# Nine more U tiles in the gate stage of a PEER layer, staged in memory, and a new pace for the gathered rows

## The chip, the cores and the metric

One core of one Trainium2 chip runs the whole program: TensorE (PE, with its weight loads shown apart as PEld), VectorE (DVE), ScalarE (ACT), GpSimd (POOL) and SyncE (SP, which here issues the plain DMAs), with 16 DMA engines shared by SP's queue and POOL's queue of gathered rows. The metric is device time in microseconds (us), median of several executions.

## The reference, cut to what matters

Two transformer blocks in a row; the change lies in the first block's PEER layer. Every token picks 16 of 16,384 experts in each of 8 heads, takes a gelu of its dot product with each expert's row of U, weights it by the gate, and sums the experts' rows of V:

```python
def peer(h, w_query, sub_keys, expert_u, expert_v):
    ...
    eidx = jnp.take_along_axis(cand_idx, pos, axis=-1)
    g = jax.nn.softmax(best, axis=-1)
    def one_block(args):
        xb, ib, gb = args
        u = expert_u[ib]
        a = jax.nn.gelu(jnp.einsum('thkd,td->thk', u, xb).astype(jnp.float32), approximate=False)
        w = (gb * a).astype(expert_v.dtype)
        return jnp.einsum('thk,thkd->td', w, expert_v[ib])
```

T is 512 tokens, D is 1024.

## The kernel before, in words

The program runs four phases: a (mixers of the first block), b (PEER), c and d (the second block). The diff touches phase b alone, `phase_b` (L887 on) with `peer_gates` (L1056 on).

For 384 of the 512 tokens (ND = 3 blocks of 128) the layer is computed densely. The 16,384 experts are cut into 128 tiles of 128. A **U tile** n is the gelu of U's tile times the tokens: the tile's weights are loaded (L227, `w_raw`, three buffers), split into two halves on ACT and DVE (L71 `w_hi`, L72 `w_lo`, two buffers each), and give 24 matmuls (8 chunks of D by three products of halves, L76 to L78, into `b_ups`, two PSUM buffers); ACT's gelu (L919) then writes the 128x384 activations. The first NX = 10 of them go into the room of x, the others into a pool of NAB = 36 buffers (`b_a`). A **V step** n (`weighted`, then `add_rows`) multiplies the activations by the gates (L973, `b_wfull`, which reads `b_g`, loaded for four n at once from the table `b_gd` in memory), splits the product (`b_wh`, `b_wl`, four buffers) and V's tile (`b_vraw`, three buffers, into `b_vh`, `b_vl`, two buffers), and adds 18 matmuls into six PSUM sums (`b_acc`).

The last 128 tokens go by **gathered rows**: POOL gathers, for expert k of every token, the rows of U by an indirect DMA into one of four 128x1024 buffers of x (L942), and DVE takes the dot products (L949), 128 times; then the same with V's rows, which DVE adds up in `b_accg` (L959), 128 times. These 256 steps are handed out beside the loop over n: by a table of paces, PACE a step of the loop.

```python
                due += 0 if n < NX else PACE if n < 128 - NAB else 1.2
                while done < min(int(due), 256):
                    next(gs)
```

Ahead of that loop stands the **gate stage** (`peer_gates`): it finds the experts and writes the dense gate table. Its last part is 12 chunks of 32 tokens: DVE makes one-hot matrices (L1225), PE multiplies them (L1234, L1235, `g_gp`, 64 matmuls of 128x128 a chunk), ACT copies the sums out (L1237, `g_sg`, two buffers), and SP writes 2 MB a chunk to `b_gd` (L1240). The stage calls `u_tile` 52 times on its way. After 46 tiles the buffers are all taken; tiles beyond that can be multiplied only as far as PSUM holds them until an old activation has been used.

Within each engine the build's scheduler sets the order of instructions from the program's order and its dependencies; gathered-row steps are kept in program order on DVE. The queues of SP, POOL, ACT and DVE run strictly in that order, so a waiting instruction holds those behind it.

Of the kernel before, what the change touches and what calls it, by code (L numbers as in the profile page):

```python
# [10 lines left out]
F32 = mybir.dt.float32  # L11
# [38 lines left out]
def bcast_rows(ap, n, parts=128):  # L50
    return bass.AP(tensor=ap.tensor, offset=ap.offset, ap=[[0, parts], [1, n]])
# [804 lines left out]
TD = ND * 128  # L856
# [3 lines left out]
NX = 10  # L860
NAB = 36
NLAST = 4
PACE = 2.72


def consts_b():
# [20 lines left out]
def phase_b(K):  # L887
    nc, tc, d = K.nc, K.tc, K.d
    V, S, PE = nc.vector, nc.scalar, nc.tensor
    with ExitStack() as st:  # L890
        pb = st.enter_context(tc.tile_pool(name="b_pb", bufs=1))
        hT = K.hT
        h2g = K.h2g
        eg = pb.tile([128, 128], I32, name="b_eg")
        gg3 = pb.tile([128, 128], F32, name="b_gg3")
        ag = pb.tile([128, 128], F32, name="b_ag")
        accg = pb.tile([128, 1024], F32, name="b_accg")
        ups = st.enter_context(tc.tile_pool(name="b_ups", bufs=2, space=PSUM))
        small = st.enter_context(tc.tile_pool(name="b_small", bufs=1))
        P = Proj(K, st, ups, pools=(K.ur, K.us))  # L900
        ab = st.enter_context(tc.tile_pool(name="b_ab", bufs=NAB))
        dram = st.enter_context(tc.tile_pool(name="b_dram", bufs=1, space=DRAM))
        gd = dram.tile([32, 128, TD // GT, 4 * GT], F32, name="b_gd")
        xd = K.xd
        room = K.x[:].rearrange("p b n -> p (b n)")

        acts = []

        def u_tile():
            n = len(acts)  # L910
            if n == 128:
                return
            hi, lo = P.weight(d["u"][n // 2, :, n % 2].rearrange("p k e -> p (k e)"))
            ps = ups.tile([128, NB, 128], F32, name="b_ups")[:, 0:ND].rearrange("p b n -> p (b n)")
            for k in range(8):
                ks = slice(k * 128, (k + 1) * 128)
                K.mm3(ps, (hi[:, ks], lo[:, ks]), (hT[0][:, k, :TD], hT[1][:, k, :TD]), k == 0, k == 7)
            a = room[:, n * TD:(n + 1) * TD] if n < NX else ab.tile([128, TD], F32, name="b_a")[:]
            S.activation(a, ps, AF.Gelu)  # L919
            acts.append(a)  # L920

        with ExitStack() as s1:
            peer_gates(K, s1, P, hT, small, gd, eg, gg3, u_tile)
        while len(acts) < NAB + NX:
            u_tile()

        with ExitStack() as s2:
            vps = s2.enter_context(tc.tile_pool(name="b_vps", bufs=1, space=PSUM))
# [36 lines left out]
            def weighted(n, halves):  # L965

                if n % 4 == 0:
                    g4s[n // 4] = gp.tile([128, TD // GT, 4, GT], F32, name="b_g")
                    nc.sync.dma_start(g4s[n // 4][:].rearrange("p c i t -> p c (i t)"), gd[n // 4])
                raw = vr.tile([128, 1024], F32, name="b_vraw")  # L970
                nc.sync.dma_start(raw[:], d["v"][n * 128:(n + 1) * 128, :])
                f = wf.tile([128, TD], F32, name="b_wfull")
                V.tensor_tensor(f[:].rearrange("p (c t) -> p c t", t=GT), acts[n].rearrange("p (c t) -> p c t", t=GT),  # L973
                                g4s[n // 4][:, :, n % 4], op=OP.mult)
                wh = wsp.tile([128, TD], F32R, name="b_wh")
                wl = wsp.tile([128, TD], F32R, name="b_wl")
                K.split(f[:], wh[:], wl[:])
                vh, vl = halves
                K.split(raw[:], vh[:], vl[:])
                return wh, wl, vh, vl  # L980

            def add_rows(n, t, b, hf):
                wh, wl, vh, vl = t
                bs, cs = slice(b * 128, (b + 1) * 128), slice(hf * 512, (hf + 1) * 512)
                K.mm3(acc[b][hf][:], (wh[:, bs], wl[:, bs]), (vh[:, cs], vl[:, cs]), n == 0, n == 127)

            def v_halves():
                return vs.tile([128, 1024], F32R, name="b_vh"), vs.tile([128, 1024], F32R, name="b_vl")

            def finish(b, xn, gf, gm, x):  # L990

                nc.sync.dma_start(x[:], xd[b])
                ss = small.tile([128, 2, 2], F32, name=f"b_fs{b}")
                y = K.x[:, b]
                for hf in range(2):
                    cs = slice(hf * 512, (hf + 1) * 512)
                    t = accg[:, cs] if b == ND else wf.tile([128, 512], F32, name="b_t")[:]
                    V.tensor_tensor(t, t if b == ND else acc[b][hf][:], K.gt2[:, cs], op=OP.mult)
                    V.tensor_tensor(x[:, cs], x[:, cs], t, op=OP.add)
                    S.activation(junk[:, cs], x[:, cs], AF.Square, scale=1 / 32, accum_out=ss[:, 0, hf:hf + 1])  # L1000
                    V.tensor_tensor(y[:, cs], x[:, cs], gf[:, cs], op=OP.mult)
                    S.activation(junk[:, cs], y[:, cs], AF.Square, scale=1 / 32, accum_out=ss[:, 1, hf:hf + 1])
                    yield
                v = small.tile([128, 2], F32, name=f"b_fv{b}")
                V.scalar_tensor_tensor(v[:, 0:1], ss[:, 0, 0:1], EPS, ss[:, 0, 1:2], op0=OP.add, op1=OP.add)
                V.scalar_tensor_tensor(v[:, 1:2], v[:, 0:1], EPS, ss[:, 1, 0:1], op0=OP.mult, op1=OP.add)
                V.tensor_tensor(v[:, 1:2], v[:, 1:2], ss[:, 1, 1:2], op=OP.add)
                V.tensor_scalar(v[:], v[:], 0.5, None, op0=OP.mult)
                r = K.rsqrt(small, v[:], 2, f"b_f{b}")
                yield  # L1010
                V.scalar_tensor_tensor(xn[:], y, r[:, 1:2], gm[:], op0=OP.mult, op1=OP.mult)
                yield
                K.turn(xn, b, hT, ups, "b_ups")
                S.activation(y, y, AF.Copy, scale=r[:, 0:1])
                yield

            gs = gather_steps()
            done, due = 0, 0.0
            last = []
            room = []  # L1020
            early = None
            for n in range(128):
                if n < 128 - NLAST:
                    t = weighted(n, v_halves())
                    for b in range(ND):
                        for hf in range(2):
                            add_rows(n, t, b, hf)
                else:
                    last.append((n, weighted(n, P.halves() if n < 130 - NLAST else v_halves())))
                if n >= NX:  # L1030
                    u_tile()
                due += 0 if n < NX else PACE if n < 128 - NAB else 1.2
                while done < min(int(due), 256):
                    next(gs)
                    done += 1
                if done == 256:
                    if early is None:
                        next(gs, None)
                        gf, gm, x = [P.raw() for _ in range(3)]
                        nc.sync.dma_start(gf[:], bcast_rows(d["g_final"], 1024))  # L1040
                        nc.sync.dma_start(gm[:], bcast_rows(d["g_mix"], 1024))
                        early = finish(ND, h2g, gf, gm, x)
                    next(early, None)
# [1270 lines left out]
def build(tc, d, out, phases="abcd"):  # L2314
# [3 lines left out]
    with ExitStack() as st:  # L2318
# [16 lines left out]
        with ExitStack() as s1:  # L2335
            if "a" in phases or "b" in phases:
                p2 = s1.enter_context(tc.tile_pool(name="p2", bufs=1))
                K.colsa = p2.tile([128, 27], F32, name="colsa")
                nc.sync.dma_start(K.colsa[:], d["colsa"])
                K.gt2 = p2.tile([128, 1024], F32, name="gt2")  # L2340
                K.A2 = p2.tile([128, 8], F32, name="A2")
                K.sh2 = p2.tile([128, 8], F32, name="sh2")
                K.h2g = p2.tile([128, 1024], F32, name="h2g")
                K.ur = s1.enter_context(tc.tile_pool(name="ur", bufs=3))
                K.us = s1.enter_context(tc.tile_pool(name="us", bufs=2))
                K.xd = s1.enter_context(tc.tile_pool(name="xd", bufs=1, space=DRAM)).tile([NB, 128, 1024], F32, name="xd")
            if "a" in phases:
                phase_a(K)
            elif "b" in phases:
                nc.sync.dma_start(K.gt2[:], bcast_rows(d["gt2_t"], 1024))  # L2350
                nc.sync.dma_start(K.A2[:], d["A2_t"])
                nc.sync.dma_start(K.sh2[:], d["sh2_t"])
            if "b" in phases:
                phase_b(K)
# [28 lines left out]
```

## Time and profile before

| | us |
|---|---|
| median of 3 runs | 2638.91 (2637.82 to 2639.2) |
| the profiled execution's own time | 2639.42 |
| its span in the trace | 2637.6 |
| gate stage, from the first key scores to the last g_gp matmul (PE) | 352 to 724 |
| from there to the first V matmul, PE idle | 724 to 740.6 |
| V loop with U tiles | 740.6 to 1430 |
| V loop without U tiles, to the last V matmul | 1430 to 1607 |

Times in the rows further below are us from the span's start. A matmul's shown length is longer than the spacing at which PE takes the next one, so the cost of a tile is read from start to start. "Idle <- X" names what ended an engine's idle time.

### The profile page before, as it was taken

To read this page: it belongs to the slowest core of one execution; us is meant where nothing else is said; L and a number is where in the kernel's file an instruction comes from. 1 tells how busy PE (TensorE), PEld (TensorE's weight loads), DVE (VectorE), ACT (ScalarE), POOL (GpSimd) and SP (SyncE) were. 2 spreads that over 40 slices of the span, in tenths; PEclk is the share of its full clock that TensorE was granted. 3 is DMA by queue.
4 is the path that set the end of the run, shared out by engine and by line. 5 is a ranking of instruction groups with operands and counts; after the bars stand their busy time and mean duration, and the time that the engine had idled before them with its cause. 6 is when DMAs were issued, how large, how long until landed. Compare 5 with 4: busy or idle time off the path is not lost. (4 is left out here: it accounts for less than half of the span.)

```text
span 2637.6 us, 43720 instructions
## 1 busy us (share of the span) xinstructions
PE 2491.0 (94%) x17112; PEld 2075.5 (79%) x17112; DVE 1784.1 (68%) x3778; ACT 919.6 (35%) x1607; POOL 379.6 (14%) x261
## 2 busy tenths in 40 slices
PE   6999999999879999999999998999999989989995
PEld 5887988998869999999998787888797856565554
DVE  6654789988847777878888997576753673333334
ACT  4532533455533333333333344343532412121112
POOL 0000000000004555545555420000000000000000
PEclk8999999999989999999999998898999999999998
DMA  6237122338868999998998973222133489999995
GB/s 244 73 115 241 57 92 81 112 118 253 244 237 300 328 323 322 330 325 314 328 327 322 353 269 117 80 81 72 62 115 116 179 328 401 409 404 386 400 390 213
DMA packets 183483, 623.92 MB, mean 237 GB/s; under 512 B 15846, under 2 KB 66406, under 8 KB 156650
## 3 DMA queue, kind: packets, MB, share of 16 engines
q1 hardware_dynamic: 146410, 486.87, 49.6%
q0 software_dynamic: 36864, 134.23, 14.6%
q8 instruction: 135, 2.21, 0.3%
q14 instruction: 74, 0.61, 0.1%
HBM read 591.55 MB, written 29.49 MB: 235 GB/s over the span
## 5 line engine op out<-in xcount | busy, mean ns | idle before, releaser
L72 DVE TENSOR_TENSOR w_lo<-w_raw,w_hi 128x1024 fp32r<-128x1024 f32 x228 | 278.2, 1220 | 250.1 <-ACT w_hi L71 247.0
L71 ACT CAST w_hi<-w_raw 128x1024 fp32r<-128x1024 f32 x228 | 238.5, 1046 | 579.5 <-issue 205.6
L78 PE MATMUL b_ups<-hT,w_lo 128*128 128x384 f32 x1024 | 347.3, 339 | 6.7 <-DVE w_lo L72 6.5
L76 PE MATMUL b_ups<-hT,w_hi 128*128 128x384 f32 x1024 | 349.6, 341 | 1.4 <-ACT x_sb L919 1.0
L77 PE MATMUL b_ups<-hT,w_hi 128*128 128x384 f32 x1024 | 346.2, 338 | 0.0
L942 POOL DMA_INDIRECT x_sb<-in_u_rows,b_eg x128 | 191.9, 1499 | 979.9 <-ACT b_wh L71 741.2
L76 PE MATMUL b_acc<-b_vh,b_wh 128*128 128x512 f32 x756 | 295.7, 392 | 17.7 <-ACT b_vh L71 17.7
L77 PE MATMUL b_acc<-b_vl,b_wh 128*128 128x512 f32 x756 | 296.7, 392 | 2.9 <-DVE b_vl L72 2.7
L78 PE MATMUL b_acc<-b_vh,b_wl 128*128 128x512 f32 x756 | 295.9, 391 | 0.0
L76 PE MATMUL p_acc<-w_hi,hT 128*128 128x256 f32 x896 | 256.4, 286 | 3.0 <-ACT hT L71 2.8
L77 PE MATMUL p_acc<-w_lo,hT 128*128 128x256 f32 x896 | 253.5, 283 | 1.4 <-DVE w_lo L72 1.3
L78 PE MATMUL p_acc<-w_hi,hT 128*128 128x256 f32 x896 | 253.1, 283 | 0.3 <-DVE hT L72 0.3
L942 POOL DMA_INDIRECT x_sb<-in_v,b_eg x128 | 187.4, 1464 | 199.6 <-DVE b_accg L959 167.0
L78 PEld LDWEIGHTS b_ups<-hT,w_lo 128*128 128x128 f32 x1024 | 194.2, 190 | 9.0 <-DVE w_lo L72 8.9
L76 PEld LDWEIGHTS b_ups<-hT,w_hi 128*128 128x128 f32 x1024 | 194.6, 190 | 6.6 <-ACT b_a L919 1.7
L77 PEld LDWEIGHTS b_ups<-hT,w_hi 128*128 128x128 f32 x1024 | 194.3, 190 | 3.0
L76 PEld LDWEIGHTS p_acc<-w_hi,hT 128*128 128x128 f32 x896 | 171.3, 191 | 18.8 <-issue 13.2
L76 PEld LDWEIGHTS b_acc<-b_vh,b_wh 128*128 128x128 f32 x756 | 142.8, 189 | 44.9 <-ACT b_vh L71 17.9
L77 PEld LDWEIGHTS p_acc<-w_lo,hT 128*128 128x128 f32 x896 | 172.0, 192 | 2.2 <-DVE w_lo L72 1.8
L1894 PE MATMUL f_hp<-f_w,f_X 128*64 128x512 f32 (+1 forms) x640 | 171.4, 594 | 0.7 <-DVE f_X L1847 0.6
L78 PEld LDWEIGHTS p_acc<-w_hi,hT 128*128 128x128 f32 x896 | 170.7, 191 | 1.4 <-DVE hT L72 0.8
L71 ACT CAST b_wh<-b_wfull 128x384 fp32r<-128x384 f32 x128 | 65.4, 514 | 298.8 <-PE b_acc L77 276.4
(660 smaller groups left out, 4916.2 us busy)
## 6 DMA issues: line engine op xcount, KB each, us to landing
f_w<-in_w SPq DMA_DIRECT2D x192, 1024.0 KB
w_raw<-in_u SPq DMA_DIRECT2D x128, 512.0 KB
b_vraw<-in_v SPq DMA_DIRECT2D x128, 512.0 KB
b_gd<-g_sg SPq DMA_DIRECT2D x12, 2048.0 KB
b_g<-b_gd SPq DMA_DIRECT2D x32, 768.0 KB
a_ar_t<-in_w_ada SPq DMA_DIRECT2D x32, 512.0 KB
w_raw<-in_w_tok SPq DMA_DIRECT2D x20, 512.0 KB
a_ar_t<-in_w_ada SPq DMA_DIRECT2D x8, 1024.0 KB
```

Of the source, the lines that this page charges most:

```text
L71: self.nc.scalar.copy(hi, src)
L72: self.nc.vector.tensor_tensor(lo, src, hi, op=OP.subtract)
L76: first = mm(ps, a[0], b[0], start=start, stop=False)
L77: mm(ps, a[0], b[1], start=False, stop=False)
L78: mm(ps, a[1], b[0], start=False, stop=stop)
L942: nc.gpsimd.indirect_dma_start(out=r, out_offset=None, in_=d[src], in_offset=bass.IndirectOffsetOnAxis(ap=eg[:, k:k + 1], axis=0))
L1894: last = PE.matmul(p, X[:, k], ts["w31", k // 2][:, c0:c0 + 512], start=k == 0, stop=k == 7, skip_group_check=True)
```

## The change

The nine tiles 46 to 54 are made by `ahead()` in the gate stage, and by a loop right behind it for those that are left: their gelu goes into one of two 128x384 pieces of `b_accg` (which the gathered rows need only much later), and SP writes each to a table `b_ud` in memory (192 KB a tile). In the V loop the steps n = 10 to 18, which used to make these tiles, read them back into a `b_a` buffer instead. The pace of the gathered rows is 1.435 a step for n = 10 to 18 and 2.87 up to n = 91, where it was 2.72 throughout: at n = 92 the count due is 9 x 1.435 + 73 x 2.87 = 222.4, before 82 x 2.72 = 223.0; from there both take 1.2 a step.

```diff
@@ -860,7 +860,8 @@
 NX = 10
 NAB = 36
 NLAST = 4
-PACE = 2.72
+NS = 9
+PACE = 2.87
@@ -905,24 +906,49 @@
         acts = []
+        first = NAB + NX
+        ud = dram.tile([NS, 128, TD], F32, name="b_ud")
+        ready = iter(range(NS))
+
+        def ahead():
+
+            i = next(ready, None)
+            if i is not None:
+                a = accg[:, i % 2 * TD:(i % 2 + 1) * TD]
+                product(first + i, a)
+                nc.sync.dma_start(ud[i], a)
 
         def u_tile():
             n = len(acts)
             if n == 128:
                 return
+            a = room[:, n * TD:(n + 1) * TD] if n < NX else ab.tile([128, TD], F32, name="b_a")[:]
+            if first <= n < first + NS:
+                nc.sync.dma_start(a, ud[n - first])
+            else:
+                product(n, a)
+            acts.append(a)
+
+        def product(n, a):
             hi, lo = P.weight(d["u"][n // 2, :, n % 2].rearrange("p k e -> p (k e)"))
...
-            a = room[:, n * TD:(n + 1) * TD] if n < NX else ab.tile([128, TD], F32, name="b_a")[:]
             S.activation(a, ps, AF.Gelu)
-            acts.append(a)
+
+        def filler():
+            if len(acts) < first:
+                u_tile()
+            else:
+                ahead()
 
         with ExitStack() as s1:
-            peer_gates(K, s1, P, hT, small, gd, eg, gg3, u_tile)
-        while len(acts) < NAB + NX:
+            peer_gates(K, s1, P, hT, small, gd, eg, gg3, filler)
+        while len(acts) < first:
             u_tile()
+        for _ in range(NS):
+            ahead()
@@ -1029,7 +1055,7 @@
                 if n >= NX:
                     u_tile()
-                due += 0 if n < NX else PACE if n < 128 - NAB else 1.2
+                due += 0 if n < NX else PACE / 2 if n < NX + NS else PACE if n < 128 - NAB else 1.2
```

The scheduler moves more than these lines say. **ACT at the end of the gate stage** (`g_sg` is the copy of gate sums, `w_hi` the split of a U weight, `b_accg` as a target is a gelu of `ahead`). Before:

```order
L1237 ACTIVATE g_sg<-g_gp 128x128x4 x4
L71 CAST w_hi<-w_raw 128x1024
L1237 ACTIVATE g_sg<-g_gp 128x128x4 x18
L71 CAST b_wh<-b_wfull 128x384 x2
L71 CAST b_vh<-b_vraw 128x1024
```

With the change:

```order
L1263 ACTIVATE g_sg<-g_gp 128x128x4 x4
L71 CAST w_hi<-w_raw 128x1024
L938 ACTIVATE b_accg<-b_ups 128x384
L1263 ACTIVATE g_sg<-g_gp 128x128x4 x2
L71 CAST w_hi<-w_raw 128x1024
L938 ACTIVATE b_accg<-b_ups 128x384
L71 CAST w_hi<-w_raw 128x1024
L938 ACTIVATE b_accg<-b_ups 128x384
L71 CAST w_hi<-w_raw 128x1024
L938 ACTIVATE b_accg<-b_ups 128x384
L71 CAST w_hi<-w_raw 128x1024
L71 CAST b_wh<-b_wfull 128x384 x2
```

The 18 copies stood in one run; now a tile's split and gelu lie between each four of them, and three more tiles behind the last. On PE the last 144 gate matmuls stood in one run, with the V matmuls right behind; now they stand as four times 32, each with a U tile of 24 matmuls behind it, then 16, then four U tiles and 16 matmuls of a fifth, and only then the first V matmul. So 8 and two thirds U tiles more stand ahead of the V loop (before, 48 stood there, two of them past the 46 buffers). Behind it come 21 V steps without a U tile, then one U tile a step up to n = 92; before, U tiles began after 5 and a half V steps and ended at n = 86.

**SP at the hand-over to the V loop** (`b_gd` the writes of the gate table, `b_ud` the writes of the nine tiles, `b_g` the first read of the gate table). Before:

```order
L227 DMA w_raw<-in_u 128x1024
L1240 DMA b_gd<-g_sg 128x32x128 x2
L969 DMA b_g<-b_gd 128x1536
L971 DMA b_vraw<-in_v 128x1024 x3
L969 DMA b_g<-b_gd 128x1536
```

With the change:

```order
L919 DMA b_ud<-b_accg 128x384
L227 DMA w_raw<-in_u 128x1024
L1266 DMA b_gd<-g_sg 128x32x128
L919 DMA b_ud<-b_accg 128x384 x2
L227 DMA w_raw<-in_u 128x1024
L995 DMA b_g<-b_gd 128x1536
L919 DMA b_ud<-b_accg 128x384
L997 DMA b_vraw<-in_v 128x1024 x3
L995 DMA b_g<-b_gd 128x1536
```

The first loads of V stand behind the ninth write of `b_ud` as well.

**DVE where the U tiles end** (`w_lo` is a U weight's split, `b_accg<-x_sb` a gathered-row step, `b_vl` the split of V, one a V step). Before:

```order
L72 TENSOR_TENSOR w_lo<-w_raw,w_hi 128x1024
L959 SCALAR_TENSOR_TENSOR b_accg<-x_sb,b_ag,b_accg 128x1024 x2
L72 TENSOR_TENSOR b_wl<-b_wfull,b_wh 128x384
L959 SCALAR_TENSOR_TENSOR b_accg<-x_sb,b_ag,b_accg 128x1024
L72 TENSOR_TENSOR b_vl<-b_vraw,b_vh 128x1024
L959 SCALAR_TENSOR_TENSOR b_accg<-x_sb,b_ag,b_accg 128x1024
L973 TENSOR_TENSOR b_wfull<-b_a,b_g 128x384
L959 SCALAR_TENSOR_TENSOR b_accg<-x_sb,b_ag,b_accg 128x1024 x2
L72 TENSOR_TENSOR b_wl<-b_wfull,b_wh 128x384
L973 TENSOR_TENSOR b_wfull<-b_a,b_g 128x384
L72 TENSOR_TENSOR b_vl<-b_vraw,b_vh 128x1024
L959 SCALAR_TENSOR_TENSOR b_accg<-x_sb,b_ag,b_accg 128x1024 x3
```

With the change:

```order
L72 TENSOR_TENSOR w_lo<-w_raw,w_hi 128x1024
L985 SCALAR_TENSOR_TENSOR b_accg<-x_sb,b_ag,b_accg 128x1024 x2
L72 TENSOR_TENSOR b_wl<-b_wfull,b_wh 128x384
L985 SCALAR_TENSOR_TENSOR b_accg<-x_sb,b_ag,b_accg 128x1024
L72 TENSOR_TENSOR b_vl<-b_vraw,b_vh 128x1024
L985 SCALAR_TENSOR_TENSOR b_accg<-x_sb,b_ag,b_accg 128x1024
L999 TENSOR_TENSOR b_wfull<-b_a,b_g 128x384
L72 TENSOR_TENSOR b_wl<-b_wfull,b_wh 128x384
L999 TENSOR_TENSOR b_wfull<-b_a,b_g 128x384
L72 TENSOR_TENSOR b_vl<-b_vraw,b_vh 128x1024
L985 SCALAR_TENSOR_TENSOR b_accg<-x_sb,b_ag,b_accg 128x1024
```

Before, up to three row steps a V step went on for some V steps after the last `w_lo`; now they drop to one in the step after it. At the other end, the ten V steps n = 11 to 20 of the change hold 16 row steps and no `w_lo` on DVE, and n = 21 to 24 hold 2, 2, 3 and 4 row steps, with a `w_lo` from n = 23 on.

## Rows read from the trace of the kernel before

**Rows 1.** Windows by stretch: length; busy PE, PEld, DVE, ACT, POOL; clock, DMA share, GB/s

```profile
707.00:724.00 17.00, 11.77 (x145) 9.63 (x143) 13.89 (x22) 10.44 (x19) 0.00 (x0) 0.90 0.86 254
724.00:740.60 16.60, 0.00 (x0) 0.00 (x0) 2.39 (x5) 1.88 (x3) 0.00 (x0) 0.55 0.87 285
740.60:747.00 6.40, 6.26 (x15) 4.51 (x16) 4.76 (x8) 1.93 (x3) 2.52 (x2) 0.56 0.93 339
...
765.00:1430.00 665.00, 664.85 (x3378) 605.81 (x3377) 519.46 (x663) 234.23 (x324) 319.09 (x209) 1.00 0.88 315
1430.00:1480.00 50.00, 47.25 (x199) 37.95 (x198) 44.12 (x46) 14.22 (x20) 25.38 (x21) 0.97 0.93 345
```

**Rows 2.** Windows of the tile b_ups alone, up to the first V matmul

```profile
440.00:740.60 300.60, 215.71 (x1152) 203.76 (x1152) 0.00 (x0) 22.33 (x46) 0.95 0.57 180
```

**Rows 3.** Timeline of PE in the V loop: start, length, engine, line

```profile
1202.48 0.34 PE L76 MATMUL b_ups<-hT,w_hi 128*128 128x384 f32 x1
...
1206.64 0.39 PE L76 MATMUL b_acc<-b_vh,b_wh 128*128 128x512 f32 x1
...
1210.73 0.34 PE L76 MATMUL b_ups<-hT,w_hi 128*128 128x384 f32 x1
```

**Rows 4.** Timeline of ACT in the gate stage's chunks with U tiles

```profile
674.03 1.05 ACT L71 CAST w_hi<-w_raw 128x1024 fp32r<-128x1024 f32 x1 [2.69 <-PE b_ups L77]
...
680.10 1.05 ACT L71 CAST w_hi<-w_raw 128x1024 fp32r<-128x1024 f32 x1 [2.69 <-PE b_ups L77]
```

**Rows 5.** Timeline of PE: the first gate matmul behind the last U tile

```profile
706.90 0.23 PE L1234 MATMUL g_gp<-g_o,g_oj 128*128 128x128 f16 x1
```

**Rows 6.** Timeline of SP's issues at the hand-over

```profile
716.75 7.29 SPq L1240 DMA_DIRECT2D b_gd<-g_sg  x2
733.64 0.33 SPq L969 DMA_DIRECT2D b_g<-b_gd  x1
734.02 1.77 SPq L971 DMA_DIRECT2D b_vraw<-in_v  x3
```

**Rows 7.** Timelines of DVE and of PE at the hand-over

```profile
738.05 1.03 DVE L973 TENSOR_TENSOR b_wfull<-x_sb,b_g 128x384 f32<-128x384 f32 x2 [16.16 <-DMA b_g<-b_gd]
...
740.62 1.65 PE L76 MATMUL b_acc<-b_vh,b_wh 128*128 128x512 f32 x3 [17.71 <-ACT b_vh L71]
```

**Rows 8.** Timeline of DVE in one step of the V loop

```profile
1207.79 1.23 DVE L72 TENSOR_TENSOR w_lo<-w_raw,w_hi 128x1024 fp32r<-128x1024 f32 x1 [2.32 <-ACT w_hi L71]
1208.94 2.60 DVE L959 SCALAR_TENSOR_TENSOR b_accg<-x_sb,b_ag,b_accg 128x1024 f32<-128x1024 f32 x2
1211.45 0.56 DVE L72 TENSOR_TENSOR b_wl<-b_wfull,b_wh 128x384 fp32r<-128x384 f32 x1
...
1213.12 1.22 DVE L72 TENSOR_TENSOR b_vl<-b_vraw,b_vh 128x1024 fp32r<-128x1024 f32 x1
1214.25 0.56 DVE L973 TENSOR_TENSOR b_wfull<-b_a,b_g 128x384 f32<-128x384 f32 x1
```

**Rows 9.** Windows of 10 us, columns as in rows 1

```profile
1470.00:1480.00 10.00, 10.00 (x46) 8.29 (x45) 9.30 (x11) 3.06 (x5) 3.74 (x4) 1.00 1.00 399
1480.00:1490.00 10.00, 10.00 (x46) 8.29 (x45) 9.66 (x15) 5.16 (x8) 4.59 (x3) 1.00 0.99 374
```

**Rows 10.** Waits, 760 to 1430, then 1430 to 1610: us, times, longest

```profile
DVE b_junkg L949 <- DMA x_sb<-in_u_rows,b_eg: 10.2, 10, 2.3
DVE b_accg L959 <- DMA x_sb<-in_v,b_eg: 5.1, 7, 2.1
...
PE b_acc L77 <- DVE b_vl L72: 2.7, 2, 1.9
```

**Rows 11.** DMA: queue of gathered rows (packets, MB, share); issues with their sizes

```profile
q0 software_dynamic: 36864, 134.23, 14.6%
...
b_vraw<-in_v SPq DMA_DIRECT2D x128, 512.0 KB
...
b_g<-b_gd SPq DMA_DIRECT2D x32, 768.0 KB
```

## The prediction

> **What bounds the kernel now.** I read the windows by stretch first. From 765 to 1430 PE is busy for 664.85 of 665 us at a granted clock of 1.00, while DVE works 519 us and the DMA engines are at 0.88 [rows 1]: in the V loop PE sets the pace. The hand-over into that loop is different. From 724 to 740.6 PE does nothing, and from 740.6 to 747 the clock is at 0.56, near the lower of its two levels (1.2 instead of 2.4 GHz), after that idle stretch [rows 1]. Before that, from 707 to 724, PE is busy for 11.8 of 17 us: the U tiles have run out (their buffers are full; 46 gelus, 1152 matmuls = 48 tiles [rows 2]), and DVE, at 13.9 us, makes the gates alone. So the time to be had lies between 707 and 747, in a core that has 80 U tiles still to make.
>
> The timelines say why PE is idle there. SP ends the issue of the last two gate writes at 724.0, can issue the first read of the table only at 733.6, and then the first loads of V at 734.0 [rows 6]; DVE gets its gates at 738.05 after 16.2 us of waiting, and PE starts at 740.62 [rows 7]. The wait is one of writing the table and reading it back, which PE could fill with anything that needs neither gates nor a free activation buffer. Nine activations put into memory are such work.
>
> **The unit prices.** A U tile costs PE 1206.64 - 1202.48 = 4.16 us, a V step 1210.73 - 1206.64 = 4.09 us [rows 3]. In the gate stage a U tile with 32 gate matmuls takes 680.10 - 674.03 = 6.07 us, and ACT waits there for PE [rows 4], so PE is the bound and 32 gate matmuls cost 1.91. On DVE, from start to start: `w_lo` 1.15, a row step 2.51 / 2 = 1.255, `b_wl` with one more row step 1.67, so `b_wl` 0.42; `b_vl` 1.13; `b_wfull` at most 0.56 [rows 8]. A V step without U and rows is 2.1 us of DVE.
>
> **The sum, against the profiled execution's 2639.4 us** (the median shown, 2638.9, is 0.5 lower).
>
> 1. *Work taken out of the loop.* By the order, 8.67 more U tiles stand ahead of the first V matmul. They cost the loop 8.67 x 4.16 = 36.1 us, all on PE's path there: **-36.1**. (Not nine: two of the tiles beyond 46 were already multiplied early, and the change also draws two thirds of a tile and one more from behind the nine.)
>
> 2. *The loop starts later.* From the end of the last U tile at 706.90 [rows 5] PE now has four times 6.07, half a gate block (0.95) and 4.67 x 4.16: it would end at 751.6. The gates are late too: the last gate matmul comes at 706.9 + 24.3 + 0.95 = 732.1 and the last write about 1 us later. With the 9.6 us from the end of issue to the table's read and the 7.0 from there to PE's start [rows 6, 7] that gives 749.7. The third path is SP's: the loads of V stand behind the ninth write, whose gelu comes with the end of the third tile after the gates, 732.1 + 12.5 + 0.5 = 745.1; V took 6.6 us from issue to PE's start [rows 6, 7], which makes 751.7. ACT splits one more U weight ahead of the first gates, which I allow 0.6 for. I take a start at 752.3, against 740.6: **+11.7** (9 to 14). The three paths meet within 2 us, so none leaves a large gap.
>
> 3. *The clock.* With PE at work until 752 there is no idle stretch ahead of the V loop. From 740.6 to 747 PE started 15 matmuls [rows 1] where at 4.09 / 18 = 0.227 us it starts 28 at full clock: **-2.9**.
>
> 4. *The end of the U tiles.* From 1430 to 1480 PE started 199 matmuls [rows 1] instead of 50 / 0.227 = 220: 4.8 us lost, with PE waiting for `b_vl` [rows 10]. It is the place where V steps had lost their U tile but still carried up to three row steps: DVE 2.1 + 3 x 1.255 = 5.9 us against PE's 4.09. In the new order the U tiles last until the pace drops. **-4.8** (0 to -4.8).
>
> 5. *The new stretch without U tiles.* The 21 V steps from 752 to about 838 give PE 4.09 us a step. Steps 11 to 20 carry 16 row steps: DVE 10 x 2.1 + 16 x 1.255 = 41.1 us against PE's 40.9, even; steps 21 and 22 with two each are 0.5 us too long apiece, then U tiles are back. DVE has two V buffers of lead, which may cover all; without it the single late steps add up. **+2** (0 to 6).
>
> 6. *DMA in that stretch.* Steps 8 to 20 (53.2 us) need 13 V tiles of 0.524 MB, 13 / 4 gate reads of 0.786, eight of the nine reads of 0.197 MB, 16 gathered steps of 134.23 / 256 = 0.524 MB [rows 11] and about one U tile: 19.8 MB, or 372 GB/s. The loop's average is 315 at a share of 0.88, but 399 and 374 were reached at shares of 1.00 and 0.99 with PE busy throughout [rows 1, 9]. At 399 it costs nothing, at 315 the stretch takes 62.9 us, 9.7 more. I take **+3**, nearer to the rows at full share.
>
> The Trainium skill, in "DMA: Bandwidth & Descriptors", Specifications, gives about 358 GB/s as the limit of memory for one core. The windows of 10 us at 399 and 374 [rows 9] do not agree with it as a ceiling. By the page the stretch would take 19.8 / 0.358 = 55.3 us and term 6 would be 2.1; by the first of those rows it would be 0.
>
> Steady steps afterwards (n = 23 to 91) cost nothing: DVE 2.1 + 1.15 + 2.87 x 1.255 = 6.9 us under PE's 8.25. Their cover is 1.4 us a step; rows made DVE wait only 15.3 us in 665 [rows 10]. The writes of `b_ud` (0.197 MB each) are hidden if they land within the two U tiles between uses of the same half of `b_accg`, 12.1 us; the last gate write, ten times as large, took 9.6. The nine extra gelus and nine DMA reads replace nine gelus and nine 512 KB loads in the loop; rows on ACT show no bound there.
>
> -36.1 + 11.7 - 2.9 - 4.8 + 2 + 3 = -27.1, so 2639.4 - 27.1 = 2612.3; less the 0.5 of the median, **2612 us**. With all costs at their good ends, -36.1 + 9 - 2.9 - 4.8 = -34.8 (2604); at their bad ends, -36.1 + 14 - 2.9 + 0 + 6 + 9.7 = -9.3 (2630).
>
> **The rivals.**
>
> *A. The DMA engines hold the stretch without U tiles.* At the loop's usual 315 GB/s term 6 is 9.7, and late rows on DVE's strict queue bring term 5 to 6: 2612 + 6.7 + 4 = 2623. For it: share 0.88 as an average leaves little. Against: rows 9.
>
> *B. The staging holds ACT.* A gelu waits for the write from the same half two tiles earlier; behind it on ACT stand the gate copies. Should each write take 15 us, as it may behind 2 MB gate writes at a DMA share of 0.86 [rows 1], seven waits of 15 - 12.1 = 2.9 us could add up to 20 us ahead of the loop, some of it hidden in term 2: 2612 + 12 = 2624.
>
> *C. Slower: gathered rows become the bound of the whole loop.* A steady step now moves 0.524 + 0.524 + 0.197 + 2.87 x 0.524 = 2.75 MB in 8.25 us, 333 GB/s, where 2.72 asked for 324. If the engines cannot go beyond the 315 of rows 1, a step takes 8.73 us, and 70 steps lose 34: 2612 + 34 = 2646. The point at which the gain is eaten is 27.1 / 70 = 0.39 us a step, or 2.75 / 8.64 = 318 GB/s. Against it: the 345 of 1430 to 1480 and the rows 9, and that waits for rows are short [rows 10].
>
> *D. The change does not fill the gap:* PE starts at 752 but U tiles wait there for weights, so the gain is only what ran beside the gates. A load of U then comes later than its tile, which SP's strict order allows, as each of those loads stands behind a write that waits for a gelu. Four tiles of 4.16 lost: 2612 + 17 = 2629.
>
> **How the numbers follow.** What can be told from no change here is 0.2%, 5.3 us. The forecast has 0.76, A 0.10, B 0.05, C 0.05, D 0.04. All of the forecast, and most of A, B and D, are faster by more than 2633.6 asks for: 0.89. A, B or D with another mishap end within 0.2%: 0.06. C is slower: 0.05. The range runs from the good ends, 2604, to 2628, which takes in A and B and most of the bad ends.
>
> **What would show it.** Right: 24-matmul U tiles among the gate matmuls from 707 to 732 and behind them to 751, no PE idle of more than 2 us there and the clock at full level; the first V matmul at 751 to 753; 56.67 tiles' U matmuls before it; about 86 us to the next U tile; no hole in PE's row where the U tiles end. Wrong: ACT's gelus waiting for DMAs from `b_accg`; fewer than 18 V matmuls in 4.3 us between 790 and 840 with the DMA share at 1; or more than 8.3 us for a steady step.

## The result and the profile after

The change takes 2604.8 us (median of 4 runs, 2601.3 to 2611.0) against 2639.05 before: ratio 0.988, 95% interval 0.9859 to 0.9901. The forecast was 2612 with a range of 2604 to 2628, so sign and time came out, the time near the good end. The profiled execution took 2603.84 us, its span 2602.0 (before 2637.6).

The windows by stretch of the change come first (length; busy PE, PEld, DVE, ACT, POOL; clock, DMA share, GB/s); they answer to [rows 1].

```profile
707.00:724.00 17.00, 17.00 (x163) 16.52 (x162) 13.32 (x20) 10.16 (x18) 0.00 (x0) 1.00 0.84 260
724.00:740.60 16.60, 16.60 (x129) 16.28 (x128) 7.23 (x9) 7.23 (x12) 0.00 (x0) 1.00 0.96 287
740.60:752.00 11.40, 11.40 (x68) 11.40 (x67) 2.77 (x3) 3.92 (x5) 0.00 (x0) 1.00 1.01 318
752.00:765.00 13.00, 10.87 (x49) 8.77 (x49) 11.59 (x19) 7.04 (x10) 4.06 (x2) 1.00 0.92 355
765.00:845.00 80.00, 79.94 (x355) 66.09 (x354) 62.01 (x91) 29.34 (x40) 27.77 (x21) 1.00 0.92 337
845.00:1395.00 550.00, 550.00 (x2802) 502.79 (x2801) 458.69 (x577) 193.90 (x268) 288.30 (x195) 1.00 0.93 340
1395.00:1445.00 50.00, 50.00 (x245) 44.29 (x244) 37.33 (x40) 16.03 (x24) 19.71 (x16) 1.00 0.80 284
```

The idle stretch of [rows 1] is full of work, the clock stays at its upper level (2.4 GHz) through the hand-over, the U-free steps (765 to 845) run without a hole, and so does the place where the U tiles end (1395 to 1445, where [rows 1] had 47.25 of 50 in 1430 to 1480). The window of the U tiles' PSUM tile alone answers to [rows 2]: 1360 matmuls, or 56.67 tiles, stand ahead of the first V matmul, as forecast from the order.

```profile
440.00:754.50 314.50, 252.69 (x1360) 239.32 (x1360) 0.00 (x0) 26.65 (x55) 0.98 0.60 186
```

The first 6.4 us of the V loop, against the 15 matmuls at a clock of 0.56 that [rows 1] has for the same length from 740.6:

```profile
754.60:761.00 6.40, 6.37 (x28) 5.28 (x29) 6.04 (x10) 3.55 (x5) 2.62 (x2) 1.00 0.83 316
```

The timelines of SP, DVE and PE at the hand-over answer to [rows 6, 7].

```profile
735.40 0.43 SPq L1266 DMA_DIRECT2D b_gd<-g_sg  x1
...
745.48 0.32 SPq L995 DMA_DIRECT2D b_g<-b_gd  x1
746.90 0.32 SPq L919 DMA_DIRECT2D b_ud<-b_accg  x1
747.27 1.94 SPq L997 DMA_DIRECT2D b_vraw<-in_v  x3
...
751.68 1.03 DVE L999 TENSOR_TENSOR b_wfull<-x_sb,b_g 128x384 f32<-128x384 f32 x2 [3.94 <-DMA b_g<-b_gd]
...
754.63 1.66 PE L76 MATMUL b_acc<-b_vh,b_wh 128*128 128x512 f32 x6 [2.13 <-ACT b_vh L71]
```

SP has issued the last gate write at 735.8; it can issue the read only at 745.5, and the table is there at 751.7. PE has stood still for 2.1 us when it starts at 754.6. The next lines are the waits from 755 to 1560 (us in total, times, longest), to be read beside [rows 10]. Rows make DVE wait longer than before (32.6 us in all, where [rows 10] has 15.3 up to 1430), but nothing of it reaches PE, whose only wait there is the start itself.

```profile
DVE b_junkg L975 <- DMA x_sb<-in_u_rows,b_eg: 22.6, 31, 2.5
DVE b_accg L985 <- DMA x_sb<-in_v,b_eg: 10.0, 14, 1.6
PE b_acc L76 <- ACT b_vh L71: 2.1, 1, 2.1
```

**One table for all kernels.** A whole run scatters by 10 us and more, so the traces are compared by marks that PE sets, read from the first and last starts of its tiles. Start: first `b_ups` matmul to first `b_acc`. Loop: first to last `b_acc`. Own work: what the loop's matmuls take by [rows 3], 2304 x 4.09 / 18 = 523.5 us for V and 4.16 / 24 for each U matmul left in the loop; lost is loop less own work. Tail: last `b_acc` to the first `f_tp`, none of which the change touches. The U matmuls ahead of the loop were counted for each kernel by the window shown above. The marks of a row come from one trace; two traces of the change differ by 0.7 us in start + loop.

| kernel | median us | start | loop | own work | lost | start + loop | tail |
|---|---|---|---|---|---|---|---|
| before | 2639.05 | 297.0 | 866.2 | 856.3 | 9.9 | 1163.2 | 465.4 |
| change | 2604.8 | 310.3 | 821.2 | 820.2 | 1.0 | 1131.5 | 460.1 |
| change again (e8) | 2609.6 | 310.9 | 821.3 | 820.2 | 1.1 | 1132.2 | 464.8 |
| e1 old pace | 2623.0 | 310.9 | 839.1 | 820.2 | 18.9 | 1150.0 | 460.6 |
| e2 six tiles | 2625.4 | 310.1 | 839.8 | 831.3 | 8.5 | 1149.9 | 463.8 |
| e3 twelve tiles | 2610.1 | 313.9 | 819.9 | 814.7 | 5.2 | 1133.8 | 476.7 |
| e4 writes on ACT | 2610.4 | 312.1 | 823.8 | 820.2 | 3.6 | 1135.9 | 465.5 |
| e5 DVE load | 2610.7 | 311.0 | 823.6 | 820.2 | 3.4 | 1134.6 | 463.4 |
| e6 DMA load | 2619.4 | 309.6 | 832.4 | 820.2 | 12.2 | 1142.0 | 464.9 |
| e7 clock fill | 2640.6 | 297.0 | 865.4 | 856.3 | 9.1 | 1162.4 | 465.5 |
| e9 old pace, 5 buffers | 2611.9 | 311.9 | 830.7 | 820.2 | 10.5 | 1142.6 | 466.2 |
| e10 change, 5 buffers | 2605.7 | 310.1 | 820.8 | 820.2 | 0.6 | 1130.9 | 466.1 |
| e11 pace only | 2635.9 | 296.8 | 870.7 | 856.3 | 14.4 | 1167.5 | 464.4 |
| e12 longer clock fill | 2641.5 | 297.0 | 865.1 | 856.3 | 8.8 | 1162.1 | 458.7 |

The change gains 31.7 us up to the last V matmul: 36.1 of work out of the loop, 8.9 of lost time, less 13.3 by the later start. In the loop PE is now 1.0 us from its own work.

### The profile page after: what moved, and what is told of

It is laid out like the page before. It is cut to its first block, busy times and chain, and to the rows that moved or that the text cites. A ratio compares the mean times of both kernels' runs of the same rounds, so it can differ in the third digit from the quotient of the medians.

```text
span 2602.0 us, 43756 instructions
## 1 busy us (share of the span) xinstructions
PE 2478.9 (95%) x17112; PEld 2068.5 (79%) x17112; DVE 1784.7 (69%) x3778; ACT 918.0 (35%) x1607; POOL 368.8 (14%) x261
## 3 DMA queue, kind: packets, MB, share of 16 engines
q0 software_dynamic: 36864, 134.23, 14.4%
## 5 line engine op out<-in xcount | busy, mean ns | idle before, releaser
L968 POOL DMA_INDIRECT x_sb<-in_u_rows,b_eg x128 | 186.3, 1455 | 953.2 <-DMA b_g<-b_gd 756.9
L975 DVE SCALAR_TENSOR_TENSOR b_junkg<-x_sb,h2g 128x1024 bf16<-128x1024 f32 x128 | 156.5, 1222 | 24.2 <-DMA x_sb<-in_u_rows,b_eg 22.6
## 6 DMA issues: line engine op xcount, KB each, us to landing
f_w<-in_w SPq DMA_DIRECT2D x192, 1024.0 KB, 10.4
b_gd<-g_sg SPq DMA_DIRECT2D x12, 2048.0 KB, 10.2
```

The source lines that it names most:

```text
L968: nc.gpsimd.indirect_dma_start(out=r, out_offset=None, in_=d[src], in_offset=bass.IndirectOffsetOnAxis(ap=eg[:, k:k + 1], axis=0))
L975: tc.keep_in_program_order(V.scalar_tensor_tensor(junk[:], r, 1.0, h2g[:], op0=OP.mult, op1=OP.mult, accum_out=ag[:, k:k + 1]))
```

## The experiments

The medians of the kernel before beside each set were 2637.5 (e1 to e4), 2637.3 (e5 to e8) and 2639.9 us (e9 to e12).

### What the new pace is worth: e1, e5, e6, e9, e10, e11

**e1** puts the old pace back under the nine staged tiles.

```diff
-PACE = 2.87
+PACE = 2.72
-                due += 0 if n < NX else PACE / 2 if n < NX + NS else PACE if n < 128 - NAB else 1.2
+                due += 0 if n < NX else PACE if n < 128 - NAB else 1.2
```

> The nine staged tiles with the pace of before (2.72 row steps a V step from n = 10 on). By the order, the twelve V steps n = 11 to 22, which have no U tile, then carry 33 row steps instead of 20: DVE 12 x 2.1 + 33 x 1.255 = 66.6 us against PE's 49, and about 27 MB of transfers, 67 us at 400 GB/s. My theory (terms 5 and 6 cost nothing because the pace was halved): those steps run over by up to 17.5 us, less what two V buffers of lead cover (8): 9 to 17 us slower than the change, about 2616 us, with PE waiting on b_vl there. Rival (the staged tiles alone make the gain, the pace is idle detail): within 2 us of the change, about 2605.

Measured: 2623.0 us, ratio to before 0.9943 (0.9924 to 0.9962); lost time 18.9 us instead of 1.0, so 18.5 of the change's 31.7 us (start + loop) hang on the pace. That is a little beyond my 9 to 17; the rival falls. The waits of e1 from 795 to 905 show PE waiting for DVE, but also that DVE itself was waiting for rows (10.2 us in the same stretch of the change), which the sum over DVE's work does not hold.

```profile
DVE b_junkg L975 <- DMA x_sb<-in_u_rows,b_eg: 15.9, 14, 2.6
...
PE b_acc L77 <- DVE b_vl L72: 9.8, 6, 2.6
```

Two loads, each put alone on the change, were meant to tell DVE from DMA.

**e5** repeats the last row's multiply once a step, **e6** writes three more tiles a step.

```diff
+                if 11 <= n < 23:
+                    again(done - 1)
...
+            def again(k):
+                r = K.x[:, (nrow[0] - 1) % NB]
+                tc.keep_in_program_order(V.scalar_tensor_tensor(
+                    junk[:], r, 1.0, h2g[:], op0=OP.mult, op1=OP.mult, accum_out=ag[:, k:k + 1]))
```

```diff
+        spare = dram.tile([12, 3, 128, TD], F32, name="b_spare")
...
+                if 11 <= n < 23:
+                    for j in range(3):
+                        nc.scalar.dma_start(spare[n - 11, j], t[0][:].bitcast(F32))
```

> The change, with one extra row-step multiply on VectorE (the last gathered row once more, no transfer) in each of the twelve V steps n = 11 to 22: about 12 x 1.2 = 14.4 us more DVE work in the stretch without U tiles, no byte more. DVE is busy 45.1 of 50 us there in the change (794 to 844), so some 5 us of it fit in and two V buffers cover up to 8. Theory 1 (the old pace lost its 18 us because DVE had more row steps than fit under 4.09 us of PE): 5 to 10 us slower than the change, with PE waiting on b_vl. Theory 2 (it lost them because the gathered rows came late, DMA being full): 0 to 3 us slower.

> The change, with three writes of the step's b_wh to unused memory (3 x 0.197 MB) in each of the twelve V steps n = 11 to 22, issued from ScalarE: 7.1 MB more to move in the stretch without U tiles, about what the old pace adds in gathered rows (6.8 MB), and no DVE work. Theory 1 (DVE was the limit): 0 to 3 us slower than the change; 36 issues cost ACT about 12 us, which it has. Theory 2 (DMA was the limit): 7.1 MB at 400 GB/s are 17.7 us, less about 3 of slack at a share of 0.95 and up to 8 of lead: 6 to 15 us slower, DVE waiting for gathered rows, PE for b_vl.

Measured: e5 lost 3.4 us, 2.4 more than the change; e6 lost 12.2, 11.2 more. Both times lie where theory 2 had them: some 14 us more of DVE work cost almost nothing, and 7.1 MB more cost two thirds of their 17.7 us. The windows of 795 to 845, of e5 and then of e6:

```profile
795.00:845.00 50.00, 50.00 (x221) 40.83 (x220) 47.52 (x75) 17.11 (x23) 18.12 (x14) 1.00 0.88 307
```

```profile
795.00:845.00 50.00, 42.87 (x179) 32.74 (x178) 37.98 (x57) 14.87 (x22) 17.91 (x14) 1.00 1.02 392
```

In e5 PE is busy for all 50 us with DVE at 47.5, so theory 1 falls. In e6 PE has 7 us of holes with the DMA share at 1.02, but theory 2's path, late gathered rows, is not what its trace shows. The waits of e6 from 795 to 905:

```profile
DVE b_wl L72 <- ACT b_wh L71: 10.9, 8, 2.3
ACT b_wh L71 <- DMA b_spare<-b_wh: 9.0, 2, 4.8
DVE b_junkg L976 <- DMA x_sb<-in_u_rows,b_eg: 7.9, 8, 1.9
```

DVE waited less for rows than in the change (7.9 us against 10.2), and from 795 to 850, where the holes are, not at all. It waited for ACT's `b_wh` (10.9 us against 1.8), and ACT waited until the extra writes had landed, a median 8.9 us after their issue, and gave a buffer of `b_wh` back. So at least part of the load's cost reached PE by the buffers that it read, and not by the rows. That the loss lies in the forecast range is luck as far as the path goes; what full DMA engines cost alone is not shown. e1 itself moved only 341 GB/s at a share of 0.93 (below).

**e9** and **e10** give the gathered U rows a fifth buffer, at the old and at the new pace.

```diff
-                r = K.x[:, nrow[0] % NB]
+                i = nrow[0] % (NB + 1 if src == "u_rows" else NB)
+                r = K.x[:, i] if i < NB else accg[:]
```

> The nine staged tiles with the old pace (as e1), but the gathered U rows rotate through five buffers instead of four (accg, unused until the V rows, is the fifth). Two causes of e1's 18 us are open. Theory A (round trip): a row takes about 8 us from issue to landing, 1.2 on DVE and 0.6 until its buffer is taken again, so four buffers give 4 / 9.8 = 0.41 rows a us, as many as e1 issued (45 in 110 us), where the old pace asks for 33 in 49; with five, 0.51: the stretch of 33 rows shortens from 81 to 65 us, and the loss falls from 18 to 3 to 11 us (2608 to 2616), more GB/s in the stretch than e1's 334 to 347. Theory B (the DMA engines are simply full): rows land later with five, the time stays at 2623 and GB/s in the stretch too.

> The change itself with five row buffers. At the new pace the stretch asks for 0.35 rows a us (1.435 in 4.09) and the steady steps for 0.348 (2.87 in 8.25), below the 0.41 that four buffers give. Theory A: the fifth buffer has nothing to shorten: same as the change (first b_ups to last V matmul 1131.5 within 1.5), DVE's waits for gathered rows about halved. Rival (the rows hold the loop in places): 3 us or more faster.

Measured: e9 2611.9 us (0.9857 to 0.991 of before), lost time 10.5 instead of 18.9. One buffer more takes 8.4 us of the loss away, within the range of theory A; theory B, by which the time would stay, falls. The windows of 795 to 905, of e1 and then of e9:

```profile
795.00:905.00 110.00, 97.90 (x437) 81.61 (x437) 93.61 (x143) 34.27 (x47) 57.41 (x45) 0.97 0.93 341
```

```profile
795.00:905.00 110.00, 103.70 (x485) 87.94 (x484) 102.12 (x158) 38.79 (x53) 61.71 (x48) 1.00 0.98 373
```

DVE, DMA and PE all do more in the same 110 us, so in e1 none of them was at its end by itself. In e1 rows went round through four buffers at 45 in 110 us (the count on POOL, whose 45 spans are these issues), 0.41 a us, which is what 4 buffers give at an estimated 9.8 us a round (8.0 from issue to landing, as measured in the change, 1.2 on DVE, 0.6 until the next issue). With five, 48 went round, 0.44 a us and not theory A's 0.51, so a round took longer there, some 11.5 us by the same estimate. What stays in e9 (9.5 us over the change) is not taken apart. PE had stood still for 3.5 us ahead of its V loop, and at a clock of 0.73 it then started 21 matmuls where the change started 28 in as long a time (1.6 us):

```profile
756.30:762.70 6.40, 6.40 (x21) 5.22 (x22) 5.41 (x9) 2.25 (x4) 2.42 (x3) 0.73 0.90 297
```

For the rest, DVE (busy for 102.1 of 110 us) and the DMA engines (at a share of 0.98) both stand open.

In e10 the fifth buffer changes nothing that can be told (1130.9 against 1131.5 and 1132.2; 2605.7 us), though DVE's waits for rows from 795 to 905 fall from 10.2 to 2.4 us. So the change's pace lies under what four buffers carry, and e10 (0.9819 to 0.9902 of before) cannot be told from it.

**e11** puts the new pace into the kernel before, without a staged tile.

```diff
-PACE = 2.72
+PACE = 2.87
-                due += 0 if n < NX else PACE if n < 128 - NAB else 1.2
+                due += 0 if n < NX else PACE / 2 if n < NX + 9 else PACE if n < 128 - NAB else 1.2
```

> The kernel before with the new pace alone (half pace for n = 10 to 18, then 2.87, then 1.2) and no staged tile. My theory: the pace brings nothing by itself, since every step from n = 10 on has a U tile before, 8.25 us of PE, under which 2.72 rows fit: within 3 us of before. Rival (the pace carries part of the 34 us): 10 us faster or more.

Measured: 2635.9 us, ratio 0.9984 (0.9967 to 1.0002): no change, and the rival falls. In its trace the loop lost 14.4 us, 4.5 more than before, since the U tiles still end at n = 86 there and the pace only drops at 92 (one trace; the median does not show these 4.5 us). The windows from 1430 to 1480 of e11 show where, 43.6 busy against the 47.25 of [rows 1].

```profile
1430.00:1480.00 50.00, 43.63 (x180) 34.26 (x180) 41.87 (x43) 13.36 (x17) 24.64 (x20) 0.97 0.94 331
```

### How many tiles: e2 and e3

```diff
-NS = 9
-PACE = 2.87
+NS = 6
+PACE = 2.823
```

(e2; e3 has 12 and 2.935 in their place.)

> Six staged tiles instead of nine, pace adjusted to 2.823. By the order 54 U tiles stand ahead of the first V matmul instead of 56.67. My theory (terms 1 to 3): +2.67 x 4.16 = +11.1 in the loop; PE has no work from about 741 until the gates are back, so the V loop starts at about 752 (-2.6) and at half clock (+2.9): about 11 us slower than the change, 2616. Rival (the write and read of the gate table sets the start at all events, so that only the first tiles, which fill idle time, count and the last ones only push the start): within 3 us of the change, 2605 to 2608.

> Twelve staged tiles instead of nine, pace adjusted to 2.935. By the order 58 U tiles stand ahead of the first V matmul instead of 56.67. My theory: -1.33 x 4.16 = -5.5 in the loop, but six whole U tiles now stand behind the last gates and end at about 758, and the loads of V stand behind the twelfth write on SP, so that V arrives some 7 us after that: start at about 765 instead of 754.6 (+10.4), PE idle for up to 7 us and the clock down again: 3 to 8 us slower than the change, 2608 to 2613. Rival (each staged tile brings a ninth of the 34 us): 11 us faster, 2594. Rival 2 (more tiles only trade places once the idle stretch is full): within 1.5 us of the change.

Measured, e2: 2625.4 us, 18.4 us more than the change up to the last V matmul, neither 11 nor within 3. Of these, 11.1 are the 2.67 tiles by their price. The start did not come earlier (310.1 against 310.3): in e2 ACT's split of V follows that of the gates' product without a wait, so the gates came last. And 7.5 us more are lost in the loop, most of them in two places, as the windows of e2 show.

```profile
740.00:755.00 15.00, 3.68 (x22) 3.36 (x20) 3.38 (x4) 1.81 (x3) 0.00 (x0) 0.70 1.03 321
755.00:765.00 10.00, 8.28 (x23) 6.10 (x24) 6.61 (x12) 4.45 (x8) 2.59 (x2) 0.60 0.90 326
...
830.00:840.00 10.00, 7.32 (x28) 5.64 (x28) 9.21 (x15) 2.35 (x3) 5.41 (x6) 0.90 0.98 365
```

PE has run out of tiles and stands still for 13.0 us, and the loop then begins at a clock of 0.60 (755 to 765). The second hole, a wait of 2.7 us for `b_vl`, looks like e1's in small (not tried apart): with six tiles the pace rises back at n = 16, and the U tiles return only at 842.

e3: 2610.1 us, 2.3 more than the change in the trace, 0.9886 of before (0.9866 to 0.9906), where the change run again has 0.9883. The rival of a ninth of the gain a tile (2594) is out. The 2.3 us lie between rival 2 (within 1.5) and my theory (3 to 8), and with 0.7 between two traces of one kernel they do not decide; that more tiles trade places is what the terms show. The start came 3.6 us later, not 10.4: SP issued the first V loads at 746.4, ahead of the last three writes (750.2 to 759.0), and PE went from its own U tiles to V at 757.3 without a pause. Of the 5.5 us fewer of own work 4.2 are lost again: one wait of ACT between 762 and 785, for a U weight whose split stood ahead of V's,

```profile
ACT w_hi L71 <- DMA w_raw<-in_u: 6.3, 1, 6.3
```

left PE busy for 7.8 of 10 us from 770 on, at a clock of 0.83.

### What sets the start: e4

```diff
-                nc.sync.dma_start(ud[i], a)
+                nc.scalar.dma_start(ud[i], a)
```

> The change, with the nine writes of the staged tiles issued from ScalarE's queue, so that SP can issue the reads of the gate table and the loads of V without standing behind a gelu. My theory: of the +14.0 us by which the V loop starts later, about 2 were that wait (V issued at 747.3 and landed 6.7 later, while PE's U tiles ended at 752.5); the start goes back to 752 or 753, and the time falls by 1 to 2 us, 2603. Rival (V would wait for the gates, whose read was itself slow at a full DMA share): same start of 754.6 and same time. Rival 2 (an issue holds ACT long enough to delay gelus and gate copies): 1 to 5 us slower.

Measured: 2610.4 us, 0.9887 (0.9868 to 0.9906); the start is 1.8 us later, not earlier. My theory falls. The first rival has the cause (the gates came last: ACT's split of V followed that of their product without a wait), but the start is not the same. The timelines of SP and DVE in e4:

```profile
736.87 0.43 SPq L1266 DMA_DIRECT2D b_gd<-g_sg  x1
...
748.74 0.33 SPq L995 DMA_DIRECT2D b_g<-b_gd  x1
749.12 2.09 SPq L997 DMA_DIRECT2D b_vraw<-in_v  x3
...
756.01 1.03 DVE L999 TENSOR_TENSOR b_wfull<-x_sb,b_g 128x384 f32<-128x384 f32 x2 [6.07 <-DMA b_g<-b_gd]
```

With no `b_ud` write ahead of them the V loads still stand behind the gate read on SP, and that is issued 11.4 us after the end of the last gate write's issue (9.6 in the change); the read itself takes 7.3 us to DVE (6.2 in the change). The waits of SP from 735 to 753 in e4 name the landing of that write as what the read waited for last.

```profile
SPq L995 <- DMA b_gd<-g_sg: 1.8, 1, 1.8
```

In the change the ninth write had held the V loads by 1.4 us at most (745.48 to 746.90), and the gates were ready only 0.3 us sooner than V. So the table's write and read back end last or within 0.3 us of it. But on SP the read also stands behind the load of a U weight, which was issued by 744.3 in the change and by 746.8 in e4, so that the landing held it for only 1.1 and 1.8 us more; a read ahead of that load was not tried, nor why write and read took longer in e4. By start + loop e4 is 4.4 us slower than the change, the size of rival 2, but its cause is not seen: ACT's nine issues took 0.33 to 0.35 us each. 1.8 us are the start, and 1.6 are the clock: PE stood still for 3.9 us ahead of the V loop, and e4 then started 21 matmuls where the change started 28.

```profile
758.60:765.00 6.40, 6.40 (x21) 5.23 (x22) 5.68 (x10) 2.19 (x4) 1.19 (x1) 0.73 0.84 270
```

### The clock by itself: e7 and e12

```diff
+        for _ in range(4):
+            ps = gps.tile([128, 4, 128], F32, name="g_gp")
+            pv = ps[:, 0:ND].rearrange("p b n -> p (b n)")
+            for k in range(21):
+                nc.tensor.matmul(pv, hT[0][:, k % 8, 0:128], hT[0][:, k % 8, :TD], start=True, stop=True)
```

(e7, on the kernel before; e12 has 26 in place of 21.)

> The kernel before, with 84 matmuls whose result nobody reads put on PE behind the last gate matmul, so that PE is at work in what was its idle stretch (724 to 740.6); nothing else is moved. My theory (term 3, the first 6.4 us of the V loop run at the lower clock because PE had been idle): the V loop starts at the same time, the clock there is at full level, and the last V matmul comes 2.9 us earlier: 2 to 4 us faster than before. Rival (the slow start has another cause, gates or V arriving late): no change.

> As e7, with 104 unread matmuls instead of 84: in e7 they ended 3.6 us ahead of the first V matmul, and the clock fell all the same (0.65 from 740.6 to 747). Now they end at about 743.3, so that PE stands still for less than 1 us. My theory (term 3): the clock stays at full level into the V loop, first b_ups to last V matmul falls from 1163.2 of before by 2 to 4 us. Rival (the slow start is not the idle stretch's): clock low again, or no us gained.

Measured: e7 0.9999 (0.9983 to 1.0014), e12 1.0004 (0.9989 to 1.0019). The windows 740.6 to 747 of e7 and then of e12:

```profile
740.60:747.00 6.40, 3.55 (x8) 2.84 (x9) 5.97 (x10) 3.81 (x6) 1.65 (x1) 0.65 0.92 344
```

```profile
740.60:747.00 6.40, 5.19 (x28) 4.61 (x27) 5.61 (x9) 3.82 (x6) 1.66 (x1) 1.00 0.93 368
```

e7 says nothing of the term: PE stood still for 3.3 us between its filler and the first V matmul, and the clock had fallen again. In e12 the clock is at its upper level, so the idle stretch is what lowers it. But only 1.1 us come of it by the last V matmul (1162.1 against 1163.2), not 2 to 4, and e7, whose clock had fallen, has 1162.4: a gain cannot be told. At full clock PE reaches the end of the first V tile sooner and waits 1.2 us for `b_vl`, which takes part of it back.

### The change once more: e8

> The change itself once more, for a second trace of it. In the first pair of traces 4.6 to 5.3 us of the gain lie after the V loop, where nothing was changed: from the last V matmul to the first f_tp 465.4 us before and 460.1 after. Theory 1 (that part differs from execution to execution with the clock after the loop): this trace shows another value than 460.1, by up to 10 us, while first b_ups to last V matmul stays at 1131.5 within 2. Theory 2 (something in the change shortens the part behind the loop): 460 within 1.

Measured: 2609.6 us, ratio 0.9883 (0.9833 to 0.9934); start + loop 1132.2 and tail 464.8. Theory 1 has the number. The tails of the table run from 458.7 to 476.7, and no edit is seen to order them. In the longest, e3, the clock from 1800 to 1860 was 0.65, and in the change's first trace 0.87 (e3, then the change).

```profile
1800.00:1860.00 60.00, 58.73 (x239) 39.91 (x239) 37.01 (x140) 26.61 (x74) 0.00 (x0) 0.65 0.06 21
```

```profile
1800.00:1860.00 60.00, 59.59 (x308) 40.13 (x307) 45.18 (x157) 32.25 (x82) 0.00 (x0) 0.87 0.10 36
```

That window alone does not order the tails: e1 and the kernel before both have 0.80 there, and tails of 460.6 and 465.4. So some 5 us of the first pair's 35.6 lie in a part that differs from trace to trace. By marks the change is worth 31.7 and 31.0 us in its two traces.

## Why the prediction was right

The work taken out, the later start, the clock and the hole at the end came as forecast, and the sum of -27.1 stands against a measured -31.7 up to the last V matmul. The 4.6 between them are 6.2 us of lost time, on which terms 3 to 6 were too high in sum, less 1.6 of start (term 2). Of the prediction's own signs two were missed narrowly: the first V matmul came at 754.6, not at 751 to 753, after 2.1 us of idle PE, not at most 2. The next U tile came 86.4 us later, where 86 were forecast.

- **Term 1 (-36.1) held.** 1360 matmuls ahead of the loop, and 36.1 us less of own work in it.
- **Term 2 (+11.7) was short by 1.6 to 2.3**, within its bounds: 13.3 from the first U matmul, 14.0 by the span. The step that was off is the path of the gates, put at 749.7 and measured at 754.6. The last gate write was issued by 735.8 and not by 733.1, behind a U weight's load on SP (734.3 to 735.3); from there to the read it took 9.6 us, as copied from [rows 6]; the read took 6.2 us from issue to DVE where [rows 6, 7] have 4.4. The DMA share is 1.01 from 740.6 to 752, against the 0.87 of [rows 1]. Of the three paths that were to meet within 2 us, PE's own tiles ended first, at 752.5, and gates and V came together: ACT split the gates' product at 752.28 and then waited 0.28 us for V, as its timeline shows.

```profile
752.28 0.98 ACT L71 CAST b_wh<-b_wfull 128x384 fp32r<-128x384 f32 x2 [1.49 <-DVE b_wfull L999]
753.54 1.04 ACT L71 CAST b_vh<-b_vraw 128x1024 fp32r<-128x1024 f32 x1 [0.28 <-DMA b_vraw<-in_v]
```

- **Terms 3 and 4 (-2.9, -4.8)** are together right in size: lost time fell by 8.9 us, and clock and hole are both gone from the windows. In its first 6.4 us the V loop now starts 28 matmuls instead of 15, which is term 3 as it was worked out. How the 8.9 divides is not settled: e12, with the clock kept up in the kernel before, gained 1.1 us at most.
- **Terms 5 and 6 (+2, +3) were the mis-sized ones:** the loop lost 1.0 us in all, so they cost at most that. For 5, e5 shows that even 14 us more on DVE cost only 2.4. For 6, the 372 GB/s asked of steps 8 to 20 were not needed: from 787.3 to 840.5 the change moved 321 at a share of 0.90 (V and gates can be loaded steps ahead; that this is why was not tried). Where it did need more, it had it, as the 10 us at 820 show.

```profile
820.00:830.00 10.00, 10.00 (x45) 8.27 (x45) 9.52 (x17) 4.40 (x6) 5.57 (x4) 1.00 1.02 410
```

  The Trainium skill's 358 GB/s for one core ("DMA: Bandwidth & Descriptors", Specifications) is passed here too (410), with PE full; this case does not bear it out as a ceiling.
- **What the list of costs lacked** is the round trip of a gathered row. The pace was checked against DVE's time and the engines' bytes. The number of row buffers is a third limit, worth 8.4 us of e1's 18.9 (e9), and the new pace stays under it (e10).
- **The rivals.** A: no extra 11 us; e6 does not test it, since its load held PE by way of ACT. B: no gelu waited for a write. C: a steady step moves its bytes, PE busy for 550.00 of 550 us at 340 GB/s, above the 318 at which the gain would have been gone. D: no wait for U weights at the hand-over; e3 shows one in small.
- The rest of the difference to the 2612 lies behind the last V matmul (465.4 to 460.1 us in the first pair), in work that the prediction had left as it was.

## What to carry to other kernels

Work moved into an idle stretch is worth its price in the loop only if what ran under it in the loop is moved too: here the staging without the new pace gave 13.2 of 31.7 us, and the pace without the staging nothing that can be told. Where a stretch loses its cover, check a gathered stream for the time of the engine that uses it and for its bytes, but also for buffers divided by the round trip. When a load is added to test a limit, look in the trace for what it held: e6's time fitted a theory whose path its waits do not show. And compare short marks in the trace when whole runs scatter by more than the effect.

## What was not expected of the hardware

- In e7 PE stood still for 3.3 us ahead of the V loop, and the clock was 0.65 from 740.6 to 747; in the change it stood still for 2.1 us, and the clock was 1.00 from 752 to 765.
- The same code after the loop took 458.7 to 476.7 us over fourteen traces, with the clock between 1800 and 1860 differing; what decides that was not tried.
- Gathered rows landed 8.0 us after their issue (median of 41 in the change from 795 to 905). With four buffers e1 carried 0.41 a us at a DMA share of 0.93, and a fifth buffer took 8.4 us off its loss.
- Three writes of 192 KB a step (e6), issued from ACT, kept the buffers that they read until they landed (8.9 us after issue in the median), and ACT waited 9.0 us for them.
